# Sixteen dense expert columns instead of twenty, with two more list tiles for all tokens, in a hybrid mixer and expert block

## The chip, the core and the metric

The kernel runs on one core of one Trainium2 chip. Its time is device microseconds (us) of one execution; the figure that counts is the median of several runs. Engine names are those of the profile: PE is TensorE (PEld its weight loads), DVE is VectorE, ACT is ScalarE, POOL is GpSimd, SP is SyncE, which here only issues DMAs.

## What is computed

One layer for 256 tokens of width 2048: a mixer (attention heads and a state-space group behind one input projection, then an output projection), and an expert layer. The expert layer is what the change is about:

```python
def peer_ffn(hn, w_query, sub_keys, expert_down, expert_up):
    q = (xt @ w_query).reshape(t, PEER_HEADS, 2, PEER_HALF)          # 8 heads, 2 halves
    scores = jnp.einsum('thcd,hckd->thck', q, sub_keys)              # 128 keys per half
    top_s, top_i = lax.top_k(scores, PEER_TOPK)                      # 16
    ...
    best_s, best_pos = lax.top_k(cand_s, PEER_TOPK)
    expert_idx = ...                                                 # key of half 0 * 128 + key of half 1
    gates = jax.nn.softmax(best_s, axis=-1)
    ...
        u = expert_down[idx]
        act = jax.nn.gelu(jnp.einsum('thkd,td->thk', u, xb), approximate=False)
        vv = expert_up[idx]
        return jnp.einsum('thk,thkd->td', (gb * act).astype(vv.dtype), vv)
```

Each token takes 128 of 16384 experts. An expert is one row of `expert_down` (2048 numbers), one activation, one row of `expert_up`. All is float32.

## The kernel before, in words

The expert number is a column (key of half 0, 128 of them) times 128 plus a place in the column. The kernel doesn't gather rows token by token. It builds a list of the experts that any token uses, in tiles of 128 experts, and works through the tiles with TensorE. The list has nine classes, by the quarters of the tokens (64 each) that use an expert: classes 0 and 1 (one token only, in the first or second half), 2 and 3 (several tokens, one half), 4 to 7 (two given quarters), and class 8, `LC`, for all tokens. `CAPS` says how many tiles each class has (111 in sum, not changed), `SPC` how many of them, from the front, may hold any expert.

The last `NDN` columns are dense: for them TensorE computes the activation of all 128 experts and all 256 tokens straight from a transposed copy of the weights (`dense`, tile `dn`: 16 products of 128x256 in plain float32, a Gelu, a store to `zd_dram`). List tiles behind the first `SPC` of a class hold only experts of dense columns; their activation is fetched from `zd_dram` instead of being computed from gathered rows. An expert that doesn't fit its class goes to class 8, and one that doesn't fit there to a loop at the very end (`rest_tile`), whose count is computed on the chip and is zero when all fit.

The program after the mixer, in the order in which it is written; each engine takes its own instructions strictly in the order of the program:

1. Queries: 16 products `pq` (16 matmuls of 128x256 each). Two and a half items later come the scores `sc` of that query (L896), and on VectorE the selection of the best 16 (L900 to L905) and, per head, the route: candidates, best 16 of them, expert numbers and gates (L966 to L1011). `FILL` puts dense columns between queries.
2. The dense columns. In their gaps TensorE gets the work of `listing`, a generator whose next piece is issued after every few matmuls: transposed expert numbers (`trT`, L1115, L1116), counts (`cnt`), ranks, the inverse of the list (`inv`), the number of left-over experts (`nr`, L1194). Then the first four gathers of `expert_down` rows are issued (`pump`, L1355).
3. `gates`: for four tokens at a time VectorE and GpSimd make one-hots (L1246 to L1249), TensorE multiplies them (`g`, L1256), ScalarE copies the result into the four gate buffers `big0` to `big3` (L1259). After each half of the tokens the buffers go to `g_dram` (`put`, L1264). One such step is issued after most items that follow.
4. Units C, one per tile of class 8 in front of `SPC[8]` (`unit_c`): 16 transposes `tc` (L1523) of a gathered tile, a split into two parts on ScalarE and VectorE (L1442, L1443), 48 matmuls `zc` (L1540 to L1542), a Gelu.
5. Units T for classes 2 to 7 (22 units of two tiles; `tp`, `z`). Their activations are kept by `zh`: the first in what is free of the buffer `xa`, the next eight tiles in `zr`, and from number `XZ` on in the first gate buffer (tag `b0`), which must have been stored to `g_dram` by then (`gated`).
6. Units D for classes 0 and 1, partly between units T, and then the up side (`out`, L1895): all 111 list tiles, two halves each.

The changed numbers stand at L65 to L67, L101 and L118, `zh` at L1367.

Of the kernel before, what the change touches and what calls it, by code (L numbers as in the profile page):

```python
# [18 lines left out]
P = 128  # L19
# [42 lines left out]
NCONST = K_LO + 2  # L62

NE = NK * NK
NDN = 20  # L65
NSC = NK - NDN
SPC = (15, 15, 10, 10, 6, 6, 6, 6, 20)  # L67
CAPS = (17, 17, 12, 12, 7, 7, 7, 7, 25)
LC = len(CAPS) - 1
BASE = [sum(CAPS[:k]) for k in range(LC + 1)]  # L70
# [2 lines left out]
NTS = sum(CAPS)  # L73
NDT = SPC[0] + SPC[1]
NTH = sum(SPC[2:LC])
NTD = NTS - sum(SPC)
GENERAL = True
# [20 lines left out]
ZLAG = 4  # L98
OLAG = 7
TF = 10  # L100
XZ = 16  # L101
HU = 5
GU = 9
DU = 11
# [10 lines left out]
NA = 4  # L115
TD = -3
HY = 1
FILL = (0,) * 9 + (1, 0, 0, 1, 0, 0, 0)  # L118
PLP = 3
NCX = 4  # L120
NCY = 4
# [22 lines left out]
def tile_block(ctx: ExitStack, tc: tile.TileContext, xT, w_f, w_v, w_dt, w_o, w_q, sk, dnt, down, up,  # L144
# [22 lines left out]
    g_dram = dr.tile([NE + P, T], F32, name="g_dram")  # L167
    zd_dram = dr.tile([NDN * P, T], F32, name="zd_dram")
    hn_dram = dr.tile([P, 2 * ND * T], F32, name="hn_dram")
# [754 lines left out]
    def dense(i):  # L924
        keep = {}
        for k in range(2):
            def go(raw, k=k):
                if k == 0:
                    keep["acc"] = ps_mm(f"dn{i}")
                mm_plain(keep["acc"], raw, xt, k)  # L930
                if k:
                    dn_done(i, keep["acc"])

            load_plain(dnt[i][:, k * 8:k * 8 + 8, :], f"dn{i}_{k}", go)

    def query(hc):
        keep = {}
        for k in range(2):
            def go(raw, k=k):
                if k == 0:  # L940
                    keep["acc"] = ps_mm(f"pq{hc}")
                mm_plain(keep["acc"], raw, hg(), k)
                if k:
                    q_done(hc, keep["acc"])

            load_plain(w_q[hc][:, k * 8:k * 8 + 8, :], f"pq{hc}_{k}", go)

    n_fill = 0
    for hc in range(16):
        query(hc)  # L950
        for _ in range(FILL[hc]):
            dense(n_fill)
# [154 lines left out]
    def listing():  # L1107
# [73 lines left out]
        for k in range(LC + 1):  # L1181
            o = sum(CAPS[i] - SPC[i] for i in range(k))
            n = CAPS[k] - SPC[k]
            TS(idz[:, o:o + n], idf[:, BASE[k] + SPC[k]:BASE[k] + CAPS[k]], -float(NSC * P), 0.0, op0=OP.add, op1=OP.max)
        regions()
# [104 lines left out]
    def gated(n):  # L1290
        while not gens.get("last") or len(gens["put"]) > n:
            work()
# [11 lines left out]
    s1_mark = len(items)  # L1304
    for i in range(n_fill, NDN):
        dense(i)
# [27 lines left out]
    part = {}  # L1334
# [7 lines left out]
    def regions():  # L1342
        lo_t = rot("raws", "lo", 8192)
        ring.extend(lo_t[:, 2048 * k:2048 * (k + 1)] for k in range(4))
# [20 lines left out]
        pump()  # L1365

    def zh(n, w=P):  # L1367
        if n < 8:
            return part["xa"][:, 3072 + P * n:3072 + P * n + w]
        if n < XZ:  # L1370
            return part["zr"][:, P * (n - 8):P * (n - 8) + w]
        n -= XZ
        if n == 0:
            gated(2)
        if n < 32:
            return held("zh", "b0")[:, P * n:P * n + w]
        return held("zh2", "b1")[:, P * (n - 32):P * (n - 32) + w]

    def held(name, tag, dt=F32):
        if name not in part:  # L1380
            part[name] = rot(name, tag, 4096, dt)
        return part[name]
# [6 lines left out]
    def zd(j):  # L1389
        n = dn_of[j]  # L1390
        o = max(NTH - XZ - 32, 0) * P + sum(T if kind[i] == LC else P for i, m in dn_of.items() if m < n)
        return held("zh2", "b1")[:, o:o + (T if kind[j] == LC else P)]
# [57 lines left out]
    def unit_t(k, r):  # L1450
# [20 lines left out]
        def go(hi, lo, s):  # L1471
# [19 lines left out]
            if s == 7:  # L1491
                zt = wtile([P, T], f"zt{j}")
                nc.scalar.activation(zt, z, AF.Gelu)

                def back():
                    zT = keep["z"][:, T:2 * T]
                    for i in range(2):
                        nc.tensor.transpose(zT[:, i * P:(i + 1) * P], zt[:, i * P:(i + 1) * P], ident)
                    dst_ = zh(th_of[j], T)
                    a_, b_ = SIDES[PHASE[k]][k % 2]  # L1500
                    if a_ < b_:
                        nc.scalar.activation(dst_, zT, AF.Copy)
                    else:
                        v, s_ = [x.rearrange("p (i h t) -> p i h t", i=2, h=2) for x in (dst_, zT)]
                        for h in range(2):
                            nc.scalar.activation(v[:, :, h, :], s_[:, :, 1 - h, :], AF.Copy)
                    formed.append(j)
                    formed.append(j + 1)

                after(ZLAG, back)  # L1510
# [139 lines left out]
    def fetch_form(j):  # L1650
# [10 lines left out]
        def multiply():  # L1661
            if not sparse[j]:
                z = zd(j)
                if k < 4:
                    TT(z, pg[:, 0:P], zr[:, k % 2 * P:k % 2 * P + P], op=OP.mult)
                elif k < LC:
                    for h, (g, v) in enumerate(zip(halves(k, pg), halves(k, zr))):
                        TT(z[:, 64 * h:64 * h + 64], g, v, op=OP.mult)
                else:
                    TT(z, pg, zr, op=OP.mult)  # L1670
                pgs.append(zr)
            elif k < 4:
                TT(zh(th_of[j]), zh(th_of[j]), pg[:, 0:P], op=OP.mult)
            elif k < LC:
                z = zh(th_of[j])
                for h, g in enumerate(halves(k, pg)):
                    TT(z[:, 64 * h:64 * h + 64], z[:, 64 * h:64 * h + 64], g, op=OP.mult)
            else:
                z = zc(j - BASE[LC])
                TT(z, z, pg, op=OP.mult)  # L1680
            pgs.append(pg)
            multiplied.add(j)
# [27 lines left out]
    for i, (_, k, r) in enumerate(ts_):  # L1710
        u_mark.append(len(items))
        u = unit_t(k, r)
        n = i - DU
# [449 lines left out]
```

## Time and profile before

| | |
|---|---|
| median of 3 runs | 1631.74 us (1631.34 to 1634.24) |
| the profiled execution, its own time | 1630.61 us |
| its span, first to last instruction | 1628.7 us |
| TensorE busy (matmuls), share of the span | 1580.7 us, 97% |
| VectorE busy | 1156.0 us, 71% |
| ScalarE busy | 779.5 us, 48% |
| GpSimd busy | 531.1 us, 33% |
| moved by DMA | 366.70 MB, 225 GB/s in the mean |

Times inside the program are microseconds from the start of the span. Matmuls are pipelined, so a matmul shown as 0.38 us long may be followed by the next one after 0.22 us; what a stretch of them costs is read from the starts. In a timeline, one row can stand for many equal instructions (x32), and a number in brackets is the time that the engine stood idle before the row, with what ended the wait.

### The profile page before, as it was taken

The page shows a single profiled execution, that of the slowest core. Times are in us where ns is not written, and L with a number is a line of the kernel's source. Part 1 is how long each engine was busy: PE and PEld are TensorE (multiplying, and loading weights), DVE is VectorE, ACT ScalarE, POOL GpSimd, SP SyncE. Part 2 cuts the span into 40 slices and gives each one's busy share as a digit, 9 for nine tenths or more (in the row PEclk, how much of TensorE's full clock was granted, in tenths as well). Part 3 has the DMA queues.
Part 4 walks back from the last instruction along what each step waited for, and adds up shares of the span by engine and source line. Part 5 has one row for each costly group of instructions (what it writes and reads, how often), then busy time and mean ns, then how long its engine had stood idle before and what let it go on. Part 6 is the DMA issues. An engine that isn't in the chain of part 4 may idle for free. (4 is left out here: it accounts for less than half of the span.)

```text
span 1628.7 us, 27340 instructions
## 1 busy us (share of the span) xinstructions
PE 1580.7 (97%) x10330; PEld 1402.2 (86%) x10331; DVE 1156.0 (71%) x2556; ACT 779.5 (48%) x1375; POOL 531.1 (33%) x499
## 2 busy tenths in 40 slices
PE   6999999999999999999999999999998999999997
PEld 6999978999888888889999999999975468887776
DVE  7776665864487988736645774677797457888896
ACT  6554457754111200415545566655552036667664
POOL 3001100211000000034423431455576555786851
PEclk9999999999999999999999999999999999999999
DMA  6654544667745534253294269678799998898893
GB/s 207 188 163 151 156 155 141 183 201 225 244 143 149 164 90 119 66 198 120 96 292 171 79 229 340 227 288 307 284 398 413 356 383 332 322 347 304 327 334 115
DMA packets 108808, 366.70 MB, mean 225 GB/s; under 512 B 12704, under 2 KB 48800, under 8 KB 82304
## 3 DMA queue, kind: packets, MB, share of 16 engines
q0 software_dynamic: 35504, 229.43, 37.7%
q1 hardware_dynamic: 70304, 134.23, 27.0%
q8 instruction: 83, 1.36, 0.3%
q10 hardware_dynamic: 2864, 1.24, 0.3%
q14 instruction: 53, 0.43, 0.1%
HBM read 337.24 MB, written 27.92 MB: 224 GB/s over the span
## 5 line engine op out<-in xcount | busy, mean ns | idle before, releaser
L1895 PE MATMUL out<-hi_up,p 128*128 128x512 f32 x716 | 194.0, 392 | 0.7 <-DVE p L1797 0.6
L1355 POOL DMA_INDIRECT raws<-in_down,idx x71 | 72.3, 1018 | 303.8 <-DVE colt L1196 161.9
L1895 PEld LDWEIGHTS out<-hi_up,p 128*128 128x128 f32 x716 | 133.8, 188 | 30.7 <-ACT hi_up L1828 1.5
L253 PE MATMUL dn<-xt_t,raw_dn 128*128 128x256 f32 x640 | 158.3, 383 | 0.1
L1443 DVE TENSOR_TENSOR t<-tp,t 128x512 fp32r<-128x512 f32 x176 | 120.0, 688 | 48.3 <-ACT t L1442 47.6
L1420 POOL DMA_INDIRECT raw_small<-g_dram,idx x111 | 123.5, 1113 | 43.5 <-issue 28.7
L1442 ACT ACTIVATE t<-tp 128x512 fp32r<-128x512 f32 x176 | 103.8, 602 | 59.7 <-PE tp L1465 57.0
L253 PEld LDWEIGHTS dn<-xt_t,raw_dn 128*128 128x128 f32 x640 | 115.2, 193 | 11.7 <-issue 0.5
L253 PE MATMUL pq<-hg,raw_pq 128*128 128x256 f32 x512 | 112.9, 379 | 0.0
L253 PEld LDWEIGHTS pq<-hg,raw_pq 128*128 128x128 f32 x512 | 96.3, 190 | 12.5
L1259 ACT ACTIVATE big<-g 128x128 f32<-128x128 f32 x256 | 70.8, 438 | 75.8 <-PE g L1256 75.8
L1248 POOL TENSOR_TENSOR B<-B,gi 128x512 bf16<-128x512 bf16 x64 | 69.7, 1091 | 91.1 <-DVE B L1246 89.9
L1465 PE MATMUL tp<-ident,raws 128*128 128x128 f32 x544 | 95.5, 273 | 2.2 <-DVE t L1443 2.2
L1540 PE MATMUL zc<-hnl,c 128*128 128x256 f32 x320 | 95.9, 300 | 0.0
L1828 ACT ACTIVATE hi_up<-raws 128x1024 fp32r<-128x1024 f32 x74 | 77.1, 1056 | 32.7 <-PE out L1895 29.3
L1542 PE MATMUL zc<-hnl,c 128*128 128x256 f32 x320 | 89.1, 278 | 0.0
L1541 PE MATMUL zc<-hnl,c 128*128 128x256 f32 x320 | 89.0, 278 | 0.0
L1828 ACT ACTIVATE hi_up<-rows_hn 128x1024 fp32r<-128x1024 f32 x68 | 71.1, 1059 | 34.7 <-PE out L1895 29.4
L1443 DVE TENSOR_TENSOR c<-tc,c 128x512 fp32r<-128x512 f32 x80 | 55.2, 691 | 43.3 <-ACT c L1442 43.3
L1249 DVE TENSOR_TENSOR A<-O,gi 128x1024 f16<-128x1024 bf16 x64 | 47.4, 741 | 52.0 <-PE g L1256 51.8
L1829 DVE TENSOR_TENSOR lo_up<-rows_hn,hi_up 128x1024 fp32r<-128x1024 f32 x58 | 71.2, 1234 | 13.3 <-ACT hi_up L1828 10.5
L1355 POOL DMA_INDIRECT rows_hn<-in_up,idx x48 | 63.0, 1312 | 46.7 <-DVE lo_up L1829 12.9
(540 smaller groups left out, 4628.4 us busy)
## 6 DMA issues: line engine op xcount, KB each, us to landing
raw_dn<-in_dnt SPq DMA_DIRECT2D x40, 512.0 KB, 3.9
raw_kq<-in_w_f SPq DMA_DIRECT2D x32, 512.0 KB, 3.8
raw_wo<-in_w_o SPq DMA_DIRECT2D x32, 512.0 KB, 4.5
raw_pq<-in_w_q SPq DMA_DIRECT2D x32, 512.0 KB, 3.8
g_dram<-big SPq DMA_DIRECT2D x16, 1024.0 KB, 14.7
raw_xb<-in_w_f SPq DMA_DIRECT2D x22, 512.0 KB, 4.4
raw_v<-in_w_v SPq DMA_DIRECT2D x16, 512.0 KB, 3.6
raw_z<-in_w_f SPq DMA_DIRECT2D x16, 512.0 KB, 3.8
```

The source lines that it names most:

```text
L253: nc.tensor.matmul(acc, raw[:, j * P:(j + 1) * P], mv[:, k * 8 + j, :], start=(k + j == 0), stop=(k * 8 + j == ND - 1))
L1355: g = nc.gpsimd.indirect_dma_start(out=where[what, j], out_offset=None, in_=down_rows if what == "down" else up_rows, in_offset=bass.Indir ...
L1420: nc.gpsimd.indirect_dma_start(out=dst, out_offset=None, in_=g_half if w == P else g_dram, in_offset=bass.IndirectOffsetOnAxis(ap=idx[:, 1 ...
L1442: a = nc.scalar.activation(hi, tp, AF.Copy).ins
L1443: d = nc.vector.tensor_tensor(lo, tp, hi.bitcast(F32), op=OP.subtract).ins
L1465: nc.tensor.transpose(tp[:, (2 * dd + i) * P:(2 * dd + i + 1) * P], row("down", j + i)[:, d * P:(d + 1) * P], ident)
L1540: nc.tensor.matmul(z, wh, ah[:, d, :], start=(d == 0), stop=False)
L1541: nc.tensor.matmul(z, wh, al[:, d, :], start=False, stop=False)
L1542: nc.tensor.matmul(z, wl, ah[:, d, :], start=False, stop=(d == ND - 1))
L1828: marks["act"] = nc.scalar.activation(hi, raw, AF.Copy).ins
L1829: marks["dve"] = nc.vector.tensor_tensor(lo, raw, hi.bitcast(F32), op=OP.subtract).ins
L1895: nc.tensor.matmul(oa[tt][2 * hf + c], w[:, k * P:(k + 1) * P], mv[:, c * 512:(c + 1) * 512], start=(i == starts[f, tt, hf] and mv is hi a ...
```

## The change

The dense columns become the last sixteen of 128; none of them stands between queries any more, so all sixteen follow the last query, where eighteen stood. Class 8 gets two more tiles that may hold any expert (22 of its 25), so there are 22 units C instead of 20, and of the list tiles that take their activation from `zd_dram` 15 are left of 17. The two more results of units C take the place in `xa` of four tiles of `zh`, so `zh` now keeps four tiles there, eight in `zr`, and uses the first gate buffer from number 12 on instead of 16.

```diff
-NDN = 20
+NDN = 16
 NSC = NK - NDN
-SPC = (15, 15, 10, 10, 6, 6, 6, 6, 20)
+SPC = (15, 15, 10, 10, 6, 6, 6, 6, 22)
...
-XZ = 16
+XZ = 12
...
-FILL = (0,) * 9 + (1, 0, 0, 1, 0, 0, 0)
+FILL = (0,) * 16
...
     def zh(n, w=P):
-        if n < 8:
-            return part["xa"][:, 3072 + P * n:3072 + P * n + w]
+        if n < 4:
+            return part["xa"][:, 3584 + P * n:3584 + P * n + w]
         if n < XZ:
-            return part["zr"][:, P * (n - 8):P * (n - 8) + w]
+            return part["zr"][:, P * (n - 4):P * (n - 4) + w]
         n -= XZ
         if n == 0:
             gated(2)
```

What TensorE does behind the ninth query (`pq` is a query, `sc` its scores, `dn` a dense column; a row with x8 is eight matmuls), before (-) and now (+):

```order
 L253 MATMUL pq_4945<-hg,raw_pq_1_4868 128x256 x8
 L896 MATMUL sc_4966<-big_72,qs_4878 128x128 x2
-L253 MATMUL dn_4983<-xt_t,raw_dn_0_4905 128x256 x8
-L253 MATMUL dn_4983<-xt_t,raw_dn_1_4916 128x256 x8
+L253 MATMUL pq_4983<-hg,raw_pq_0_4905 128x256 x8
+L253 MATMUL pq_4983<-hg,raw_pq_1_4916 128x256 x8
 L896 MATMUL sc_5050<-big_72,qs_4926 128x128 x2
```

The dense column is gone and the next query follows at once; the same happens at the second place of `FILL`.

TensorE around the first transposes `trT` of the list, before; `sc_5507` are the scores of the last query, and `dn_5399` the first dense column behind it:

```order
L896 MATMUL sc_5456<-big_72,qs_5346 128x128 x2
L253 MATMUL dn_5473<-xt_t,raw_dn_0_5359 128x256 x8
L253 MATMUL dn_5473<-xt_t,raw_dn_1_5370 128x256 x8
L896 MATMUL sc_5507<-big_72,qs_5380 128x128 x2
L253 MATMUL dn_5524<-xt_t,raw_dn_0_5397 128x256 x8
L253 MATMUL dn_5524<-xt_t,raw_dn_1_5431 128x256 x8
L253 MATMUL dn_5648<-xt_t,raw_dn_0_5471 128x256 x6
L1115 MATMUL trT<-ident,big_69 128x128
L253 MATMUL dn_5648<-xt_t,raw_dn_0_5471 128x256 x2
L1116 MATMUL trT<-ident,big_69 128x128
```

The same place now, where the last scores are `sc_5459`:

```order
L896 MATMUL sc_5408<-big_72,qs_5244 128x128 x2
L253 MATMUL dn_5425<-xt_t,raw_dn_0_5287 128x256 x8
L253 MATMUL dn_5425<-xt_t,raw_dn_1_5312 128x256 x8
L896 MATMUL sc_5459<-big_72,qs_5322 128x128 x2
L253 MATMUL dn_5476<-xt_t,raw_dn_0_5349 128x256 x8
L253 MATMUL dn_5476<-xt_t,raw_dn_1_5383 128x256 x8
L253 MATMUL dn_5600<-xt_t,raw_dn_0_5423 128x256 x8
L253 MATMUL dn_5600<-xt_t,raw_dn_1_5441 128x256 x4
L1115 MATMUL trT<-ident,big_69 128x128
L253 MATMUL dn_5600<-xt_t,raw_dn_1_5441 128x256 x3
L1116 MATMUL trT<-ident,big_69 128x128
```

Between the last scores and the first `trT` there were 22 dense matmuls and are now 28, and three instead of two lie between the first two `trT`.

TensorE behind `nr`, the last matmul of the list, up to the first product `g` of the gates, now (before, four rows of eight dense matmuls stood here, 32):

```order
L1194 MATMUL nr<-big_70,tb_r 128x1
L253 MATMUL dn_6847<-xt_t,raw_dn_1_6636 128x256 x2
L253 MATMUL dn_6915<-xt_t,raw_dn_0_6708 128x256 x8
L253 MATMUL dn_6915<-xt_t,raw_dn_1_6780 128x256 x8
L253 MATMUL dn_6951<-xt_t,raw_dn_0_6845 128x256 x8
L1256 LDWEIGHTS B_6924
```

All in all 146 dense matmuls lie between `trT` and `nr`, before and now; behind `nr` there were 88 and are now 50. Of these 50, 26 stand ahead of the first `g`, and 34 dense matmuls and three steps of `g` ahead of the first transposes `tc`; before, 72 dense matmuls and five steps stood there. Seven steps of `g` stand ahead of the last dense matmul in both.

## Rows read from the trace of the kernel before

**Rows 1.** Page: busy time by engine; TensorE in 40 slices, tenths.

```profile
PE 1580.7 (97%) x10330; PEld 1402.2 (86%) x10331; DVE 1156.0 (71%) x2556; ACT 779.5 (48%) x1375; POOL 531.1 (33%) x499
PE   6999999999999999999999999999998999999997
```

**Rows 2.** Windows: stretch, length, busy us (instructions) by engine, clock, DMA share, GB/s.

```profile
540.00:572.00 32.00, 29.19 (x141) 25.21 (x140) 30.67 (x160) 7.30 (x11) 0.00 (x0) 1.00 0.54 157
738.00:928.00 190.00, 190.00 (x1640) 187.70 (x1639) 118.60 (x216) 97.90 (x280) 73.34 (x68) 1.00 0.49 162
928.00:1180.00 252.00, 246.56 (x2051) 239.92 (x2050) 172.81 (x383) 155.12 (x330) 109.19 (x114) 1.00 0.75 269
1180.00:1334.00 154.00, 142.05 (x492) 88.55 (x492) 106.81 (x304) 42.30 (x76) 93.07 (x88) 0.99 0.98 386
```

**Rows 3.** Timeline of TensorE, the first dense column between queries.

```profile
481.57 7.07 PE L253 MATMUL dn<-xt_t,raw_dn 128*128 128x256 f32 x32
488.48 0.61 PE L896 MATMUL sc<-big,qs 128*128 128x128 f32 x4
```

**Rows 4.** Timeline of TensorE in units C, two items.

```profile
753.04 0.60 PE L1523 MATMUL tc<-ident,raws 128*128 128x128 f32 x4
...
754.89 1.11 PE L1256 MATMUL g<-A,B 128*128 128x128 f16 x8
755.82 0.62 PE L1523 MATMUL tc<-ident,raws 128*128 128x128 f32 x4
...
757.70 1.11 PE L1256 MATMUL g<-A,B 128*128 128x128 f16 x8
```

**Rows 5.** Timeline of VectorE, 506 to 548: its waits for scores.

```profile
506.88 0.28 DVE L905 FIND_INDEX8 slot<-slot,s 128x8 uint32<-128x128 f32 x1
510.74 0.30 DVE L900 MAX8 slot<-sc 128x8 f32<-128x128 f32 x1 [3.57 <-PE sc L896]
...
518.09 0.30 DVE L900 MAX8 slot<-sc 128x8 f32<-128x128 f32 x1 [4.49 <-PE sc L896]
...
547.05 0.30 DVE L900 MAX8 slot<-sc 128x8 f32<-128x128 f32 x1 [0.24 <-PE sc L896]
```

**Rows 6.** Timeline of TensorE, last scores to the list's transposes.

```profile
554.21 9.66 PE L253 MATMUL dn<-xt_t,raw_dn 128*128 128x256 f32 x44
565.93 0.33 PE L1115 MATMUL trT<-ident,big 128*128 128x128 f32 x1 [2.06 <-DVE big L1006]
...
567.87 0.33 PE L1116 MATMUL trT<-ident,big 128*128 128x128 f32 x1 [0.75 <-DVE big L1011]
```

**Rows 7.** Timeline of TensorE where its clock falls, and two windows there.

```profile
1237.95 0.74 PE L1609 MATMUL xe<-hnt,ot 128*128 128x512 f32 x2 [1.49 <-DVE raws L1615]
1240.55 0.33 PE L1572 MATMUL otb<-ident,raw_small 128*128 128x128 f32 x1 [1.86 <-DVE raw_small L1563]
1241.32 2.93 PE L1609 MATMUL xe<-hnt,ot 128*128 128x512 f32 x6 [0.45 <-ACT ot L1573]
...
1238.00:1242.00 4.00, 1.69 (x5) 0.97 (x6) 3.66 (x14) 1.32 (x3) 2.99 (x4) 0.91 1.02 421
1242.00:1246.00 4.00, 4.00 (x14) 3.15 (x13) 0.49 (x1) 0.93 (x1) 2.08 (x3) 0.66 1.02 414
```

**Rows 8.** End of the list: TensorE, GpSimd's second gather, its landing (DMA issues).

```profile
692.14 0.18 PE L1194 MATMUL nr<-big,tb_r 128*128 128x1 bf16 x1
696.19 1.26 POOL L1355 DMA_INDIRECT raws<-in_down,idx  x1 [0.17 <-issue]
raws<-in_down,idx POOLq DMA_INDIRECT x1, 8.8
```

**Rows 9.** Page: the gates' work on GpSimd and VectorE, and their stores to memory.

```profile
L1248 POOL TENSOR_TENSOR B<-B,gi 128x512 bf16<-128x512 bf16 x64 | 69.7, 1091 | 91.1 <-DVE B L1246 89.9
L1249 DVE TENSOR_TENSOR A<-O,gi 128x1024 f16<-128x1024 bf16 x64 | 47.4, 741 | 52.0 <-PE g L1256 51.8
...
g_dram<-big SPq DMA_DIRECT2D x16, 1024.0 KB, 14.7
```

## The prediction, made before the changed kernel ran

> **What bounds the kernel now.** I read the page first: TensorE is busy for 97% of the span, the next engine for 71%, and the row of 40 slices shows TensorE at nine tenths or more in nearly all of them [rows 1]. So the first question to each edit is how much TensorE time it takes away or adds. Busy time alone doesn't say that TensorE is the limit, so I then took windows by stage. In units C TensorE is busy for all of 190 us, VectorE for 118.60; in units T for 246.56 of 252; the memory queues have room in both (shares 0.49 and 0.75). Only from 1180 to 1334 does DMA stand at 0.98 with TensorE at 142.05 of 154 [rows 2]. Where the list begins it is different again: from 540 to 572 VectorE is busy 30.67 of 32 us, and TensorE waits there [rows 2, 6]. So two places can answer otherwise than TensorE's sum: the start of the list, where VectorE is late, and the stage after 1180.
>
> **Dense columns taken away.** A dense column stands from 481.57 to the next row at 488.48: 6.91 us, or 0.432 us for each of its 16 matmuls [rows 3]. Four are gone, two between the queries and two behind them: 4 x 6.91 = 27.6 us less for TensorE.
>
> **Units C added.** A unit is four items; an item without a gate step is four transposes and twelve products, from 753.04 to 754.89 and from 755.82 to 757.70, 1.85 and 1.88 us [rows 4]. Two units are 8 x 1.865 = 14.9 us. The gate steps between them (0.93 us each, 754.89 to 755.82) don't become more, they only move forward from units T. The upper bound is the stage's mean, 190 us over 20 units, 9.5 us and 19.0 for two, which counts gate steps twice; I take 14.9, since TensorE is busy through the whole stage and the starts say what one item costs.
>
> **The wait in front of the list.** Here something is given back. The first `trT` needs the route of the last head from VectorE, and already before TensorE waits 2.06 us for it and 0.75 us at the second [rows 6]. Without the two dense columns TensorE comes here earlier, but VectorE has the same selection and routing to do. TensorE: the dense work behind the last scores begins at 554.21 - 2 x 6.91 = 540.4, and 28 matmuls now stand ahead of `trT`: 28 x 0.432 = 12.1, so it arrives at 552.5. VectorE: it gains only where it had waited for scores. It is done with one set at 507.2 and waits until 510.74 for scores that now come 6.91 earlier, so this wait of 3.57 goes. The next scores come 6.91 us earlier too, so VectorE then starts at 511.2 instead of 518.09, and of the 4.49 us of waiting 3.3 go; behind the second dense column the scores are 13.8 us ahead and VectorE, 6.9, never catches up with them, so the last 0.24 goes as well [rows 5]. Together about 7.2 us, and `trT` can start at 565.93 - 7.2 = 558.7. TensorE waits 6.2 us at the first `trT`; the second has one matmul more in front (0.43), which leaves 0.3. That is 6.5 us of waiting instead of 2.8: 3.7 us given back. Bounds: if VectorE gains nothing, `trT` stays at 565.93, the wait is 13.4 and 11.2 us are given back; if it is early, nothing is given back, and the 2.8 of now is won. Behind the waiting matmul stands all of TensorE's further work; the counts of the list follow from it, so nothing else is late.
>
> **The clock.** At 1237.95 and 1240.55 TensorE had stood idle for 1.49 and 1.86 us; after it the granted clock is 0.91 and then 0.66 in windows of 4 us, so 3.4 us at 1.2 GHz instead of 2.4: (0.09 + 0.34) x 4 / 0.5. Six matmuls took 2.93 us there [rows 7]. At the wait of 2.06 us in front of the list it did not fall: the stretch from 540 to 572 shows 1.00 [rows 2, 6]. A wait of 6.2 us is longer than either, so I count with the fall, and 3.4 us at half speed cost 1.7; I take 1.5, between 0 and 1.7. The Trainium skill (TensorE: Matmul & The Clock Gate, Why this matters for your kernels) asks to leave no longer gaps of idle time between bursts of matmuls, because the clock then goes back to half; it speaks against this change, and this trace agrees at 1241, not at 566. By the rule the sum below is -6.8 us, and without this term -8.3.
>
> **Less cover behind the list.** `nr` ends the list at 692.14; the first gathers follow, and the second lands 8.8 us after its issue at 696.19, at 705 [rows 8]. Before the first transposes of a gathered tile there now stand 34 dense matmuls and three gate steps: 34 x 0.432 + 3 x 0.93 = 17.5 us instead of 72 x 0.432 + 5 x 0.93 = 35.8. The transposes would start at about 709.6 on the old clock, still behind the landing of the first two gathers, so this costs nothing; if the first tile landed later, the delay would be paid in full. The gate steps do bunch: seven of them now share 50 dense matmuls, 21.6 us, with the first transposes. A step needs 0.741 us and two shorter operations on VectorE and 1.091 us on GpSimd [rows 9]; in the mean there are about 2.4 us per step (21.6 us and seven times 0.93, less the 11.2 us of 26 matmuls ahead of the first, over seven). I take 0.7 us for the two that follow each other directly, between 0 and 3.
>
> **The rest at nothing.** The first gate buffer is needed two units T earlier. But the gates now run beside eight more items of units C and end in the first unit T instead of the third. In the program's order the buffer's last store is issued early in the third unit T (before: in the fourth), and the first result goes there behind the seventh (before: the ninth). Four units lie between, at 252 us for 22 [rows 2] some 45 us, and a store lands in 14.7 us [rows 9]. Two fetches from `zd_dram` fewer, of 128 KB each, are 0.7 us at the 386 GB/s of the stage from 1180 [rows 2] if they stood on its path; I take 0. Class 8 needs its two tiles: worked out from the reference's inputs, 2,502 of its experts lay outside the dense columns before and 2,700 lie there now, which 20 tiles (2,560) don't hold and 22 (2,816) do; so the loop at the end still runs zero times.
>
> **The sum.** -27.6 + 14.9 + 3.7 + 1.5 + 0.7 = -6.8 us. The profiled execution took 1630.61 us, 1.9 more than its span and 1.1 less than the median of 1631.74. So I expect 1623.8 us for a profiled execution and 1624.9 us for the median.
>
> **Rivals.**
> - No new wait in front of the list (VectorE keeps up, or the program's order hides it): -27.6 + 14.9 = -12.7, 1619 us. Against it: VectorE is busy 30.67 of 32 us there [rows 2]. Chance 0.15.
> - The gain is swallowed: either VectorE regains nothing and gives back 11.2 (1630.2 us), or the stage from 1180, with DMA at 0.98, ends when its bytes are moved and not when units T end. For the second speaks the share; against it, that tiles there are gathered only as units T give buffers free, so that the stage's start moves with them. About 1630 us; chance 0.16.
> - Slower: the gate steps without cover. If each of the eight around the last dense matmuls waited for its chain, VectorE 0.741 and two shorter operations, GpSimd 1.091 and the product 0.93 us one behind the other [rows 4, 9], some 2 us each of waiting, 16 us would be lost and the time be 1641. It decides from 1.3 us a step (8 x 1.3 = 10.1 = 6.8 + 3.3). Against it: in units C the same steps come every 2.8 us (754.89 to 757.70) with TensorE never idle [rows 2, 4]. Chance 0.06.
> - The forecast's case, a wait between 4 and 9 us in front of the list: 1622 to 1628 us, chance 0.58. The remaining 0.05 is for things not seen, on the side of faster.
>
> **How the numbers follow.** A measurement of this kernel tells about 0.2%, 3.3 us, from no change. Faster by more than that: 0.58 + 0.15 + 0.05 = 0.78; within it 0.16; slower 0.06. The range goes from the first rival, 1619 less half a microsecond, to the second, 1630: 1618.5 to 1630.
>
> **What would show it.** In the profile after: 512 dense matmul rows, 32 for each of sixteen columns, and 352 for each line of `zc` instead of 320; a wait of about 6 us at the first `trT` at about 559, put down to L1006, with a granted clock under 1.00 right behind it; TensorE without gaps through units C; the last dense matmul 27.6 less 5.9, about 22 us earlier than before. The forecast is wrong if the wait is under 2 or over 10 us, if TensorE shows gaps at the gate products behind the list, or if the stage after 1180 grows by what was won ahead of it.

## The result, and the profile after

The changed kernel took 1622.59 us (median of four runs, 1621.16 to 1624.92) against 1631.86 for the kernel before on the same chip: ratio 0.9942, 95% interval 0.9925 to 0.9959, or 9.3 us less (6.7 to 12.2). Forecast were 6.8 us less, 1624.9 us. The profiled execution of after took 1624.92 us, 1623.0 of it in the span; it is the slowest of the four, and its first 410 us, which the change does not touch, lost 1.3 us (3.4 us at half clock near 316 us). Where starts are compared below, these 1.3 us are in them. The ratios below leave out three executions that took far longer than the others of their kernel: 1734.8 us (fifteen columns), 1953.93 (the kernel before, on the chip of the quicker lists) and 5383.25 (two columns between, quicker).

The page of after, the lines that answer to [rows 1]:

```profile
PE 1572.8 (97%) x10330; PEld 1397.0 (86%) x10331; DVE 1162.7 (72%) x2564; ACT 775.2 (48%) x1375; POOL 526.3 (32%) x499
...
PE   6999999999999999999999999999998999999997
```

TensorE is busy 7.9 us less. In the windows by stage, which answer to [rows 2] (start of list, list, units C, units T, the stage bound by DMA), TensorE has no gap in 210 us of units C. This stretch is 20 us longer than before, because besides eight items it took six gate steps from units T; the stretch of units T is 6 us shorter:

```profile
540.00:568.00 28.00, 22.47 (x101) 19.22 (x100) 25.80 (x117) 4.34 (x8) 0.00 (x0) 0.88 0.43 129
568.00:688.00 120.00, 118.80 (x811) 102.62 (x811) 98.64 (x288) 24.84 (x43) 0.00 (x0) 1.00 0.29 91
717.00:927.00 210.00, 210.00 (x1811) 207.37 (x1810) 132.00 (x242) 108.76 (x314) 81.28 (x76) 1.00 0.48 157
927.00:1173.00 246.00, 242.90 (x2009) 237.08 (x2008) 164.84 (x365) 149.92 (x306) 102.12 (x108) 0.99 0.77 276
1173.00:1334.00 161.00, 149.09 (x515) 93.49 (x514) 112.16 (x310) 45.67 (x79) 96.72 (x92) 0.98 0.97 384
```

In front of the list, TensorE's timeline (start, length, then the wait ahead of an instruction in brackets) answers to [rows 6]:

```profile
541.69 12.25 PE L253 MATMUL dn<-xt_t,raw_dn 128*128 128x256 f32 x56
559.47 0.48 PE L1115 MATMUL trT<-ident,big 128*128 128x128 f32 x1 [5.53 <-DVE big L1006]
559.74 2.77 PE L253 MATMUL dn<-xt_t,raw_dn 128*128 128x256 f32 x6
562.30 0.42 PE L1116 MATMUL trT<-ident,big 128*128 128x128 f32 x1
```

And four windows of the same place (the last three columns are the granted clock, the share of DMA and GB/s):

```profile
552.00:556.00 4.00, 1.94 (x10) 1.36 (x8) 3.93 (x35) 0.51 (x2) 0.00 (x0) 1.00 0.45 135
556.00:560.00 4.00, 0.53 (x2) 0.53 (x3) 4.00 (x5) 0.00 (x0) 0.00 (x0) 0.60 0.00 0
560.00:564.00 4.00, 4.00 (x13) 3.21 (x13) 2.01 (x7) 0.29 (x1) 0.00 (x0) 0.55 0.01 4
564.00:568.00 4.00, 4.00 (x22) 3.48 (x21) 3.86 (x15) 1.37 (x2) 0.00 (x0) 1.00 0.66 196
```

(In the rows of the kernel before, the first dense column behind the last scores is `dn_5524`, not `dn_5399`.) TensorE is out of work at 553.9 and waits 5.53 us for L1006, VectorE's reduction that gives expert numbers of the last head. The granted clock falls in the wait itself: (0.40 + 0.45) x 4 = 3.4 us of full speed are missing in the second and third window, so about 6.8 us passed at 1.2 GHz, some 2.7 of them in the wait and 4.1 behind it (the clock is 0.76 in the mean of the wait and 0.54 from its end to 564). There six rows (three matmuls) of a dense column last 559.74 to 562.30 where 1.30 us would be usual, and the transposes behind them take twice their time: 1.7 us lost.

Behind the list (the same view, against [rows 8]) there is no wait for a gathered tile, and 0.36 us for ScalarE, which empties the gate products:

```profile
686.49 0.18 PE L1194 MATMUL nr<-big,tb_r 128*128 128x1 bf16 x1
686.52 11.47 PE L253 MATMUL dn<-xt_t,raw_dn 128*128 128x256 f32 x52
697.83 1.10 PE L1256 MATMUL g<-A,B 128*128 128x128 f16 x8
...
704.09 0.94 PE L1523 MATMUL tc<-ident,raws 128*128 128x128 f32 x7
705.39 1.10 PE L1256 MATMUL g<-A,B 128*128 128x128 f16 x8 [0.36 <-ACT big L1259]
```

### The profile page after: what moved, and what is told of

The parts are those of the page before. It is cut to its first block, busy times and chain, and to the rows that moved or that the text cites. A ratio compares the mean times of both kernels' runs of the same rounds, so it can differ in the third digit from the quotient of the medians.

```text
span 1623.0 us, 27318 instructions
## 1 busy us (share of the span) xinstructions
PE 1572.8 (97%) x10330; PEld 1397.0 (86%) x10331; DVE 1162.7 (72%) x2564; ACT 775.2 (48%) x1375; POOL 526.3 (32%) x499
## 5 line engine op out<-in xcount | busy, mean ns | idle before, releaser
L1443 DVE TENSOR_TENSOR t<-tp,t 128x512 fp32r<-128x512 f32 x176 | 120.3, 688 | 52.4 <-ACT t L1442 51.8
L1420 POOL DMA_INDIRECT raw_small<-g_dram,idx x111 | 120.1, 1082 | 45.2 <-issue 28.5
L253 PE MATMUL dn<-xt_t,raw_dn 128*128 128x256 f32 x512 | 131.5, 387 | 0.1
L1540 PE MATMUL zc<-hnl,c 128*128 128x256 f32 x352 | 105.6, 300 | 0.0
L253 PEld LDWEIGHTS dn<-xt_t,raw_dn 128*128 128x128 f32 x512 | 92.3, 196 | 9.0 <-issue 0.5
L1828 ACT ACTIVATE hi_up<-raws 128x1024 fp32r<-128x1024 f32 x78 | 81.4, 1056 | 36.4 <-PE out L1895 34.7
L1542 PE MATMUL zc<-hnl,c 128*128 128x256 f32 x352 | 98.1, 279 | 0.0
L1541 PE MATMUL zc<-hnl,c 128*128 128x256 f32 x352 | 98.0, 278 | 0.0
L1443 DVE TENSOR_TENSOR c<-tc,c 128x512 fp32r<-128x512 f32 x88 | 60.7, 690 | 45.3 <-ACT c L1442 45.2
L1355 POOL DMA_INDIRECT rows_hn<-in_up,idx x48 | 66.3, 1381 | 53.0 <-DVE lo_up L1829 14.3
L1895 PE MATMUL out<-lo_up,p 128*128 128x512 f32 x254 | 76.9, 395 | 1.7 <-DVE lo_up L1829 1.7
```

What stands on the lines that cost most here:

```text
L253: nc.tensor.matmul(acc, raw[:, j * P:(j + 1) * P], mv[:, k * 8 + j, :], start=(k + j == 0), stop=(k * 8 + j == ND - 1))
L1355: g = nc.gpsimd.indirect_dma_start(out=where[what, j], out_offset=None, in_=down_rows if what == "down" else up_rows, in_offset=bass.Indir ...
L1420: nc.gpsimd.indirect_dma_start(out=dst, out_offset=None, in_=g_half if w == P else g_dram, in_offset=bass.IndirectOffsetOnAxis(ap=idx[:, 1 ...
L1443: d = nc.vector.tensor_tensor(lo, tp, hi.bitcast(F32), op=OP.subtract).ins
L1540: nc.tensor.matmul(z, wh, ah[:, d, :], start=(d == 0), stop=False)
L1541: nc.tensor.matmul(z, wh, al[:, d, :], start=False, stop=False)
```

## The experiments

Each kernel was timed against the kernel before on its own chip; times below are medians, and us against the kernel before unless another is named.

**All columns behind the queries.** The kernel before with one edit, so that TensorE's work is the same:

```
-FILL = (0,) * 9 + (1, 0, 0, 1, 0, 0, 0)
+FILL = (0,) * 16
```

> The kernel before, with its twenty dense columns all behind the queries (none between them) and nothing else changed; TensorE's work is the same to the matmul. Theory (VectorE is late in front of the list, so TensorE that comes sooner waits longer, and its clock falls behind the wait): the wait at the first trT grows from 2.8 us to about 5.5, the granted clock stands under 1.00 around it, and the time rises by 2.7 for the wait and 1.8 for the clock, +4.5 us (between +3 and +6). Rival 1 (TensorE's order hides it, no new wait): 0 us. Rival 2 (VectorE regains nothing): the wait is 13.4 us and the time rises by 11 us or more.

Measured: 1640.03 against 1634.12, +5.9 us (ratio 1.0039, 1.0025 to 1.0053). The wait in TensorE's timeline is that of after, and the windows around it miss as much clock:

```profile
558.83 0.48 PE L1115 MATMUL trT<-ident,big 128*128 128x128 f32 x1 [5.53 <-DVE big L1006]
```

```profile
552.00:556.00 4.00, 1.30 (x7) 0.80 (x5) 3.93 (x29) 0.51 (x2) 0.00 (x0) 0.96 0.39 131
556.00:560.00 4.00, 1.17 (x4) 0.99 (x5) 4.00 (x4) 0.00 (x0) 0.00 (x0) 0.50 0.00 0
560.00:564.00 4.00, 4.00 (x16) 3.35 (x15) 1.99 (x9) 0.38 (x1) 0.00 (x0) 0.69 0.03 6
```

That is 2.7 of new waiting and 1.7 of clock, the theory's price, and inside the interval of 4.1 to 8.7 us; both rivals are out. Where the columns stand costs some 4 to 6 us although the work is the same. What lies between 4.4 and 5.9 is not settled; in units T this trace has 6.8 us at half clock (near 1065 and 1164), and the kernel before has none there.

**The added units alone.** The kernel before with the new gate buffer's split and 22 units C:

```
-SPC = (15, 15, 10, 10, 6, 6, 6, 6, 20)
+SPC = (15, 15, 10, 10, 6, 6, 6, 6, 22)
```

> The kernel before with two more units C and with the gate buffer's first activations moved as in the change, but with all twenty dense columns in their old places: the added work alone. Theory (TensorE is busy throughout the stage, an item costs its own transposes and products): 8 items of 1.865 us, +14.9 us (between +13.5 and +16.5). Rival 1 (an item costs the mean of its stage): +19.0 us. Rival 2 (the stage that is bound by DMA at the end absorbs it): under +10 us.

Measured: 1646.27 against 1634.12, +12.2 us (ratio 1.0075, 1.0062 to 1.0089). The interval, 10.1 to 14.5, overlaps the theory's bounds but leaves out 14.9, and 19.0 with it; the second rival's limit of 10 it misses narrowly. Windows of this kernel for units C and units T, and then of the kernel before for units T:

```profile
739.00:948.00 209.00, 209.00 (x1806) 206.38 (x1805) 131.69 (x241) 108.35 (x313) 80.72 (x76) 1.00 0.48 158
948.00:1195.00 247.00, 243.97 (x2020) 238.13 (x2018) 165.71 (x366) 150.85 (x307) 103.35 (x108) 0.99 0.77 276
```

```profile
927.30:1180.80 253.50, 248.06 (x2065) 241.42 (x2063) 174.24 (x383) 156.17 (x331) 110.47 (x114) 1.00 0.75 269
```

Units C grew from 188.8 us (738.5 to the last product at 927.3) to 209.1, by 20.3; six gate steps of 0.93 us moved in, which leaves 14.7 for eight items: the term was right, and the forecast for the whole kernel was not. The difference lies in units T. There TensorE stood idle for 5.4 us before (253.50 less 248.06) and for 3.0 now, with 7 gate steps left in the stage instead of 13. The prediction had put that at nothing.

**Two columns between the queries kept.** The changed kernel with the old places:

```
-FILL = (0,) * 16
+FILL = (0,) * 9 + (1, 0, 0, 1, 0, 0, 0)
```

> The changed kernel, but with two of its sixteen dense columns between the queries as before, so that fourteen stand behind them. Theory (the place of the columns matters at both ends of the list): the wait at the first trT is 2 to 3 us again and the clock stays, but behind nr only 8 dense matmuls and one gate step, some 4.4 us, are left ahead of the first transposes of a gathered tile, and that tile lands about 10.4 us behind nr; so a wait of about 6 us comes there, with 1.8 for the clock and 0.7 for gate steps. Against the kernel before: -12.7 + 8.5 = -4.2 us (between -7 and -1), and so some 5 us slower than the changed kernel. Rival (the wait in front of the list is the only loss of the change): -12.7 us against the kernel before.

Measured: 1623.49, -10.6 us (ratio 0.9935, 0.9922 to 0.9949): nearer the rival, and the same as the changed kernel. The wait in front is 2.1 + 0.7 us again at a clock of 1.00, and the waits behind `nr` did come, but smaller than I had worked out:

```profile
691.98 0.18 PE L1194 MATMUL nr<-big,tb_r 128*128 128x1 bf16 x1
692.02 3.70 PE L253 MATMUL dn<-xt_t,raw_dn 128*128 128x256 f32 x16
696.47 1.10 PE L1256 MATMUL g<-A,B 128*128 128x128 f16 x8 [0.75 <-DVE A L1249]
700.15 1.09 PE L1523 MATMUL tc<-ident,raws 128*128 128x128 f32 x8 [2.58 <-DMA raws<-in_down,idx]
```

```profile
700.00:704.00 4.00, 3.85 (x21) 3.20 (x22) 3.15 (x7) 1.09 (x2) 3.13 (x4) 0.68 0.43 175
704.00:708.00 4.00, 4.00 (x29) 3.70 (x27) 3.31 (x6) 2.86 (x12) 1.77 (x3) 0.89 0.80 266
```

The tile is there 8.2 us behind `nr`, not 10.4. Behind it the clock fell (0.68 and 0.89 in the windows from 700 to 708, or 3.4 us at half speed). So 3.3 us of waiting and 1.7 of clock stand behind the list, where after has 2.7 and 1.7 in front of it: the loss changed its place and kept its size. Against the kernel with the added units alone, from which only the four columns differ, it is 22.8 us less: 27.6 for four columns, less the 5.0 lost behind the list; in front of it the two differ by 0.6 us.

**The wait filled.** The changed kernel with twelve dense matmuls more ahead of `trT`; the last line stands around its transposes:

```
-YR = 2
-YC = 2
-YT = 2
+YR = 1
+YC = 0
+YT = 16
...
+            marks_pe[0] = nc.tensor.matmul(acc, raw[:, j * P:(j + 1) * P], mv[:, k * 8 + j, :], start=(k + j == 0), stop=(k * 8 + j == ND - 1)).ins
...
+            with tc.issue_after(marks_pe[0]):
```

> The changed kernel with twelve dense matmuls more ahead of the first trT and as many fewer behind it (the transposes are traced later and held behind the matmul that was traced last; the rests of the list's steps are shorter), so 72 instead of 60 behind the last query; TensorE's work is the same. Theory (5.5 us of waiting and 1.8 of clock are lost in front of the list and can be filled): the wait at the first trT goes under 1 us, the clock stays at 1.00 there, nr comes 6 to 7 us sooner than in the changed kernel; behind nr 26 dense matmuls and two gate steps are left, 13.1 us against a landing 10.4 us behind nr, which still covers. Against the kernel before -9.3 - 5.5 - 1.8 = -16.6, plus 0 to 2 for the thinner cover: -15.6 us (between -17 and -13). Rival (VectorE sets the list's end, the wait only moves to a later step of the list): about -9 us as in the changed kernel.

Measured: 1622.85, -11.3 us (ratio 0.9932, 0.9918 to 0.9945). The theory fell, though the interval (-13.4 to -9.0) touches the edge of its bounds. The waits at `trT` are down to 0.4 and 1.6 us and the clock stays, but `nr` is only 2.0 us sooner than in after (684.53), 1.5 counted from the first query. VectorE sets where `trT` can start: 17.9 us behind the last product of the scores, filled or not (559.05 less 541.15; in after 559.47 less 541.58). And the twelve matmuls are missing later:

```profile
559.05 0.33 PE L1118 MATMUL trT<-ident,big 128*128 128x128 f32 x1 [0.36 <-DVE big L1008]
560.97 0.33 PE L1119 MATMUL trT<-ident,big 128*128 128x128 f32 x1 [1.59 <-DVE big L1013]
...
684.53 0.18 PE L1197 MATMUL nr<-big,tb_r 128*128 128x1 bf16 x1
684.57 11.47 PE L255 MATMUL dn<-xt_t,raw_dn 128*128 128x256 f32 x52
...
702.65 1.04 PE L255 MATMUL dn<-xt_t,raw_dn 128*128 128x256 f32 x4
707.04 1.11 PE L1259 MATMUL g<-A,B 128*128 128x128 f16 x8 [3.35 <-DVE A L1252]
```

```profile
704.00:708.00 4.00, 0.96 (x9) 0.99 (x9) 3.66 (x8) 0.00 (x0) 1.18 (x2) 0.79 0.00 0
708.00:712.00 4.00, 4.00 (x20) 3.35 (x19) 3.90 (x6) 2.54 (x9) 2.49 (x2) 0.50 0.00 0
712.00:716.00 4.00, 4.00 (x20) 3.40 (x19) 1.53 (x4) 0.37 (x1) 0.19 (x1) 0.85 0.00 0
```

A new wait of 3.35 us for VectorE at a gate product, and half clock with it (0.79, 0.50 and 0.85 in the windows from 704 to 716, 6.9 us in all): what was won in front is paid behind. The last dense matmul starts at 715.16, against 715.65 in after. I had taken the filled wait off the list's end, but the list could not begin sooner.

**A quicker list.** Is it TensorE's order that sets the list's length? The next four went to one chip: the changed kernel once more, the filled one with a quicker pace, the one with two columns between, and the changed kernel with a quicker pace. The edit is the first line below; in the filled kernel the inverse has it too, by the others.

```
-CR = 2.0
+CR = 2.5
...
-IR = 1.0
+IR = 1.15
...
-            while c0 < NK and credit >= 1 and len(q) < 2:
+            while c0 < NK and credit >= 1 and len(q) < 3:
```

> The changed kernel itself, once more, so that the others of this group have it on the same chip. From the first comparison: -9.3 us against the kernel before, between -12 and -7.

> The filled kernel with a quicker list: 2.5 instead of 2.0 count steps and 1.15 instead of 1.0 inverse steps are released for each call between TensorE's matmuls (and three instead of two inverse steps may be under way), so that 134 dense matmuls instead of 142 stand between trT and nr, and 50 instead of 42 behind nr, 34 of them and four gate steps ahead of the first gathered tile. Theory (the dense matmuls are cover that was too small for both ends of the list as long as TensorE set the list's pace; VectorE had 20% idle in it): the wait at trT stays at 2.0 us, nr comes 3 to 4 us sooner than in the filled kernel, the 3.3 us of waiting behind it and the clock's fall go, and the time is 5 us under the filled one, -16 us against the kernel before (between -18 and -13). Rival (VectorE sets the list's pace): nr where it was, waits inside the list instead, -11 us.

> The kernel with two dense columns between the queries (fourteen behind) and the quicker count steps (2.5 instead of 2.0), so that 139 dense matmuls instead of 146 stand between trT and nr and 31 instead of 24 behind it. Theory: in front of the list it waits 2.8 us as before the change; behind nr 15 dense matmuls and a gate step, 7.4 us, stand ahead of the first gathered tile instead of 4.4, so its wait of 2.6 us and the fall of the clock go nearly: 4 to 5 us under the same kernel with the old pace, -15 us against the kernel before (between -17 and -12). Rival (VectorE sets the list's pace): -11 us.

> The changed kernel with the quicker count steps alone (2.5 instead of 2.0): 133 dense matmuls between trT and nr, 63 behind it. Theory (its loss is the wait in front of the list, which the pace behind it doesn't touch, and behind nr it waits 0.4 us only): nr 5 us sooner, more cover than is needed, and the time of the changed kernel within 1 us, -9 to -10 us against the kernel before. Rival (a sooner end of the list is worth its own time): -14 us.

Measured, against 1646.97 on this chip: the changed kernel 1636.08 (ratio 0.9928, 0.9907 to 0.9950), filled and quicker 1635.91 (0.9928, 0.9901 to 0.9955), two columns between and quicker 1638.68 (0.9943, 0.9922 to 0.9963), the changed kernel quicker 1641.44 (0.9964, 0.9947 to 0.9982). None beats the changed kernel. The two that combine the pace with other edits fit their rival's 11 us (intervals -16.3 to -7.4 and -12.8 to -6.1); the last is 5 us behind the changed kernel and missed theory and rival. From the first `trT` to `nr` these traces have 126.9, 126.7, 126.7 and 126.9 us, and the earlier ones 126.2 (before), 127.0 (after), 126.2 (two columns between) and 125.5 (filled): 133 to 146 dense matmuls in this stretch, and nearly the same length. In the changed kernel with the quicker pace TensorE waits in front of the inverse (timeline), and the clock falls there (windows):

```profile
641.08 0.26 PE L1220 MATMUL inv<-iA,iB 128*128 128x111 bf16 x1 [2.94 <-DVE iA L1231]
```

```profile
640.00:644.00 4.00, 2.56 (x24) 2.42 (x24) 3.53 (x12) 2.34 (x4) 0.00 (x0) 0.52 0.18 71
644.00:648.00 4.00, 3.71 (x29) 2.88 (x28) 3.86 (x12) 2.50 (x6) 0.00 (x0) 0.50 0.11 34
```

The list is as long as with the old pace, and the thirteen dense matmuls that it lost (5.6 us) now stand behind `nr`: these make the 5 us. So the mechanism of the first two's rival was right as far as it was tried: the list's length does not follow the pace of TensorE's order. One part stays open: the 56 dense matmuls among the counts (54.0 to 54.1 us in all these traces) did not change with this edit, so that stretch was not tried.

**One column more or less.** Seventeen with one between the queries and 21 units C, as below; fifteen by `NDN` alone; eighteen with 21 units C and two between the queries, by the same three lines (`NDN`, `SPC`, `FILL`):

```
-NDN = 16
+NDN = 17
-SPC = (15, 15, 10, 10, 6, 6, 6, 6, 22)
+SPC = (15, 15, 10, 10, 6, 6, 6, 6, 21)
-FILL = (0,) * 16
+FILL = (0,) * 12 + (1, 0, 0, 0)
```

> Seventeen dense columns, one of them between the queries (behind the thirteenth), and 21 units C, which by the counts of the inputs still hold class 8 (2,648 experts outside the dense columns, 2,688 places). Theory (from the last scores to the first gathered tile a chain of fixed length runs through VectorE and the gathers, some 126.5 us of it from trT to nr; sixteen columns are about one too few to fill it, and what TensorE has too little it waits): -20.7 for three columns, +7.3 for one unit C, -1.2 for waits in units T that go as gate steps move ahead, and the waits around the list no larger than before the change (2 to 3 us in front, none behind, no fall of the clock there): -15 us against the kernel before (between -17 and -12). Rival (the chain doesn't bind, each column counts in full and the waits stay those of the changed kernel): 7 us less gain for the column and 7.3 more for the unit, -9.5 us as with sixteen.

> Fifteen dense columns, all behind the queries, and the 22 units C of the change (2,777 experts outside, 2,816 places): one dense column fewer than the changed kernel and nothing else. Theory (the chain binds at sixteen): the 6.9 us are not won; the wait at trT stays at 5.5 us, and behind nr 18 dense matmuls and one gate step, 8.7 us, are left ahead of the first gathered tile, so that 2 to 4 us of waiting come there and at the gate products, with the clock's fall: -10 us against the kernel before (between -12 and -8). Rival (no bound yet): -16 us.

> Eighteen dense columns, two of them between the queries as before the change, and 21 units C. Theory: the waits around the list are those of the kernel before (2.8 us in front, none behind), and so the plain sum holds: -13.8 for two columns, +7.3 for one unit, -1.2 for waits in units T: -7.7 us against the kernel before (between -10 and -5).

Measured, against 1633.29: seventeen 1623.20, -10.1 (ratio 0.9935, 0.9913 to 0.9957); fifteen 1620.24 (0.9923, 0.9906 to 0.9939, so -12.6 by the ratio), between its theory's 10 and its rival's 16; eighteen 1627.85, -5.4 (0.9968, 0.9955 to 0.9981), inside its bounds. Seventeen misses its 15 for two reasons that the trace shows. Units T stand idle for 6.1 us there, with ten gate steps in them, where 1.2 less than the 5.4 of before were expected. (In the trace of eighteen they stand idle for 6.9, with ten steps too.) The rival's 9.5 fits by its number alone: the waits at `trT` are 2.1 and 0.7 us, not those of the changed kernel. And in units C a wait is new: ScalarE can't empty the first products of the gates' second half until the first half has been stored from the same buffer. Its timeline with seventeen columns, and then TensorE's:

```profile
845.87 0.40 ACT L1259 ACTIVATE big<-g 128x128 f32<-128x128 f32 x1 [1.77 <-PE g L1256]
852.97 0.81 ACT L1259 ACTIVATE big<-g 128x128 f32<-128x128 f32 x3 [6.70 <-DMA g_dram<-big]
```

```profile
853.83 1.10 PE L1256 MATMUL g<-A,B 128*128 128x128 f16 x8 [3.33 <-ACT big L1259]
```

And ScalarE in the changed kernel, at the same store:

```profile
848.71 0.84 ACT L1259 ACTIVATE big<-g 128x128 f32<-128x128 f32 x3 [1.65 <-DMA g_dram<-big]
```

With eighteen columns ScalarE waits 4.99 and TensorE 1.6 us there. In the changed kernel ScalarE waits 1.65 us and TensorE none: it was close.

**Fifteen again.** The same kernel, for a second trace:

> The kernel with fifteen dense columns and 22 units C once more, since the profiled execution of the first time ran at a granted clock of 0.85 from its start to its end and shows nothing of the waits. It had -12.6 us against the kernel before (interval -15.4 to -10.0), between theory (-10) and rival (-16). If the chain binds, this trace shows 5.5 us of waiting at trT and some 2 to 4 us more behind nr than the changed kernel (0.4), and the last dense matmul 3 to 5 us sooner than there instead of 6.9; if not, no such waits and 6.9 us.

Measured: 1618.69 against 1633.09, -14.4 us (ratio 0.9916, 0.9900 to 0.9933). TensorE's timeline:

```profile
683.85 8.02 PE L253 MATMUL dn<-xt_t,raw_dn 128*128 128x256 f32 x36
...
692.74 1.07 PE L1523 MATMUL tc<-ident,raws 128*128 128x128 f32 x8
...
698.53 0.61 PE L253 MATMUL dn<-xt_t,raw_dn 128*128 128x256 f32 x2
701.54 2.06 PE L1256 MATMUL g<-A,B 128*128 128x128 f16 x16 [2.39 <-DVE A L1249]
```

The wait in front is 5.5 us again; 2.39 us for a gate product are new, with the clock at 0.55 and 0.60 in the windows from 700 to 708 (6.8 us at half speed). The last dense matmul starts at 709.9 against 715.7, 5.8 us sooner, of which 2.6 were there at the first query (406.7 against 409.4): 3.1 us of the column's 6.9 are won. So the list's chain and the gate steps behind it take half of the sixteenth column's worth; the theory that put the limit at sixteen was too strict.

## Why the prediction was right

- **Dense columns, -27.6.** Right: 512 rows, the last one 21.4 us sooner (22.7 without the 1.3 us lost ahead of it; about 22 forecast).
- **Units C, +14.9.** Right in size: 352 rows for each line of `zc`, and 14.7 us by the experiment with them alone.
- **The wait in front of the list, +3.7.** The mechanism is right, and both rivals to it fell: TensorE runs out at 553.9 (552.5 forecast, 1.3 us of it lost earlier), L1006 is waited for, and `trT` starts 6.5 us sooner, 7.8 without the 1.3, for 7.2 forecast. So 5.53 us instead of 6.2, and no second wait, since the six rows between the two transposes ran at half clock: +2.7.
- **The clock, +1.5.** It fell as forecast, 1.7 us lost. The rule that speaks against gaps (the Trainium skill, TensorE: Matmul & The Clock Gate, Why this matters for your kernels) agrees with the rows at 556 to 564.
- **Bunched gate steps, +0.7.** 0.36 us, and for ScalarE, which empties the products, not for VectorE and GpSimd, from which the term was built. It is also a gap at a gate product, which the forecast named as a sign of being wrong; it is small. That the cover of 17.5 us suffices was right too (17.6 from `nr` to the first `tc`, with no wait for the tile); the experiments say how nearly.
- **What was put at nothing.** Units T hold two missing terms. First, TensorE's idle time there went from 5.4 to 3.1 us, -2.3. Every kernel with 22 units C has 7 gate steps and 3.0 to 4.6 us there; those with 20 or 21 have 10 to 13 steps and 5.4 to 6.9 (traces of the chip with the quicker lists, where this stage is longer altogether, and the first trace of fifteen columns left out). The waits are nearly all for VectorE's copies (L1443). That the steps cause them is not shown, and one pair speaks against it: with all twenty columns behind the queries ten steps stand there, three fewer than before, and the idle time is 6.7 us (5.6 for these copies), not less. Second, the clock fell there once, behind a wait of 2.18 us for L1443, to half for 3.4 us (windows below); in the kernel before it did not fall in this stage. So from the last `zc` to the first `xe` it is 6.7 us less, where six steps and the 2.3 make 7.9: 1.2 us went back.

```profile
1050.00:1054.00 4.00, 2.30 (x11) 2.30 (x12) 2.69 (x6) 0.14 (x1) 1.89 (x2) 0.71 0.07 22
1054.00:1058.00 4.00, 4.00 (x30) 3.91 (x30) 3.02 (x9) 1.79 (x3) 2.49 (x3) 0.86 0.91 313
```

- **The stage from 1180** did not absorb the gain: `xe` starts 7.5 us sooner and ends 6.1 sooner, and the windows from 1232 to 1240 (0.58 and 0.57) hold 6.8 us at half clock where before there were 3.4 [rows 7].

With the measured terms the sum is -27.6 + 14.9 + 2.7 + 1.7 + 0.4 - 2.3 = -10.2, and -9.0 with the 1.2 us of clock in units T; both lie inside the interval of 6.7 to 12.2 us less. The traces agree: from the first query to the first `xe` after is 8.7 us shorter. That their spans differ by 5.7 us only comes from the 1.3 us lost ahead of the queries and another 1.3 in the stage from 1180.

The forecast has two slips that don't touch its sum. If VectorE gained nothing, the waits would be 13.4 and 0.3 us, so 10.9 given back and not 11.2; and 8 x 1.3 is 10.4, so that the slower case decides from 1.26 us a step.

## What to carry to other kernels

Work that an engine does while another finishes a chain has two values, its own time and the wait that it covers; before taking some away, measure the chain's length from end to end (here 125.5 to 127.5 us from `trT` to `nr`, with 133 to 146 dense matmuls between) and not one wait. Moving cover from one end of such a chain to the other only moves the wait, as three kernels within 2 us of each other showed (-9.3, -10.6 and -11.3 us). And a stage that an edit seems to shorten by a known amount can change its waits and its clock as well: look there too. Fifteen columns with 22 units C have the lowest ratio here, 0.9916 and 0.9923 against 0.9942 and 0.9928 for the change, but the two were not timed on one chip and the intervals overlap.

## What the runs showed of the hardware that was not expected

- The same wait at `trT`, 2.05 to 2.07 us, left the clock at 1.00 in the kernel before [rows 2, 6] and in the kernels of sixteen and eighteen columns with two of them between the queries. In three others the clock fell behind it, to half for 3.4 us: in the kernel with the added units alone, in the windows below; with seventeen columns (0.66 and 0.91 from 556 to 564); and with two columns between and the quicker pace (0.91 and 0.67 from 564 to 572). So a wait of this length may cost nothing beside itself, or up to 1.7 us. In units T it is the same: 2.3 us at a `z` left the clock at 1.00 before, 2.18 us halved it in the changed kernel.

```profile
564.00:568.00 4.00, 1.95 (x6) 1.12 (x5) 3.91 (x6) 0.00 (x0) 0.00 (x0) 0.79 0.09 38
568.00:572.00 4.00, 4.00 (x17) 3.53 (x17) 2.82 (x10) 0.38 (x1) 0.00 (x0) 0.78 0.44 131
```

- Units T of the changed kernel took 246.7 us in one trace and 262.7 on another chip, with the same matmuls and a granted clock of 0.99 in both; TensorE's idle time was 3.1 us in the one and 11.7 in the other. Why is open; it is why kernels are compared on one chip.
